# A weight ring kept past the end of the mixer, and VectorE's forming steps kept in program order

## The chip, the core and the metric

The kernel runs on one core of one Trainium2 chip. The metric is the device time of one execution in microseconds. Its engines are TensorE (PE, with its weight loads as PEld), VectorE (DVE), ScalarE (ACT), GpSimd (POOL) and SyncE (SP), which only issues transfers here.

## What is computed

One transformer layer over 512 tokens of width 1024, in float32:

```
xn = rms_norm(h);  proj = xn @ w_in
... four mixers (short conv, spatial gating, stick-breaking and forgetting attention) ...
h = h + (sum over mixers of sigmoid(gate) * (y @ w_branch)) @ w_out
g, u = split(rms_norm(h) @ w_ffn_in)        # 1024 -> 2 x 2816
h = h + (silu(g) * u) @ w_ffn_out           # 2816 -> 1024
```

The change touches the last two lines, the feed-forward part.

## The kernel before

Every matrix is held transposed, 128 rows to a tile, tokens along the free axis. A float32 product is made of three float32r products: each operand is split into a high part (ScalarE copies it, L181) and a low part (VectorE subtracts, L182), and TensorE forms high by high, high by low and low by high. Weights come in chunks of eight 128x128 units, 512 KB each. A chunk is loaded into a raw tile by a transfer on SP's queue, and split into `whi` and `wlo`, two rings of three tiles in `wpool`, which lives through the whole kernel. So ScalarE can split a chunk once TensorE is done with the chunk three before it.

**The mixer** takes its raw tiles from `rawp`, a ring of three that is opened inside the stack `mix`. Its last stage multiplies by w_out: eight output rows d, one chunk of weights each, 24 matmuls of 512 columns. After each row VectorE adds x (L766), ScalarE makes the high part for the feed-forward and the square (L770, L773), VectorE the low part and the sum of squares (L771, L774). Then `mix.close()` (L784) gives the memory of the mixer back, and two pools, `opool` and `ffn`, are opened over it.

**The feed-forward, plain stage** (L856 to L912): the first four hidden rows of 128, eight chunks. TensorE's instructions are kept in program order here. The first chunk's products with k below 6 come first, then the sums for the norm (`rms`), with the remaining products of the first row between its two steps. Between the products, `steps` of `operands` (L882) form the operands of the next stage.

**The superblocks** (L947, 13 of them): the remaining rows in 2x2 blocks by Winograd's form of Strassen's scheme, seven products instead of eight. A superblock loads four weight blocks, `b11`, `t1`, `b22`, `b21` (b11 is added into t1 by a GpSimd transfer that accumulates, L810), forms three sums of them on VectorE (L959, L971, L978) and splits seven weight operands. A product is 24 matmuls of 256 columns (L922 to L924). Nine superblocks are of kind "in" (two hidden rows each), four of kind "out". In their order, three "in" follow on each complete group of eight hidden rows before the first "out" of that group.

**The forming** makes the token operands of an "out" pair: `operands` gives eleven steps, seven that split a quarter (`operand`) and four that add or subtract quarters (`differ`, and the sum in L897). They stand in the list `forming`, and `form()` (L933) takes one at a time, at four places of each superblock. So in program order the eleven steps of a group lie over three superblocks. Program order is not what the engines run: a list scheduler arranges each engine's instructions by its own estimate of when they are ready, within the dependencies. `tc.keep_in_program_order` puts an instruction behind the instruction that was written before it on its engine.

**The end**: 48 units of w_ffn_out in plain products again (L1021), six chunks, loaded by `block` like the others.

In the feed-forward all raw tiles come from `block` (L805), a ring of six tiles named `sraw` in the pool `ffn`.

Of the kernel before, what the change touches and what calls it, by code (L numbers as in the profile page):

```python
# [11 lines left out]
F32 = mybir.dt.float32  # L12
F32R = mybir.dt.float32r
BF16 = mybir.dt.bfloat16
AF = mybir.ActivationFunctionType
ALU = mybir.AluOpType
AX = mybir.AxisListType

P = 128
# [12 lines left out]
PLAIN = 4  # L32
GROUP = 8
REST = 16

BLOCKS = 6
EPS = 1e-6
NEG = -1e30
UNITS = 8
# [84 lines left out]
def mixer_kernel(ctx, tc, xT, units, ffn_units, quads, wt1, wt2, wsT, small, out):  # L124
    nc = tc.nc
    V, S, G, PE = nc.vector, nc.scalar, nc.gpsimd, nc.tensor

    const = ctx.enter_context(tc.tile_pool(name="const", bufs=1))
    wpool = ctx.enter_context(tc.tile_pool(name="wpool", bufs=3))
    keep = ctx.enter_context(tc.tile_pool(name="keep", bufs=1))  # L130
    psum = ctx.enter_context(tc.tile_pool(name="psum", bufs=1, space=bass.MemoryType.PSUM))

    mix = ExitStack()
    fixed = mix.enter_context(tc.tile_pool(name="fixed", bufs=1))
    sm = mix.enter_context(tc.tile_pool(name="sm", bufs=4))
    rawp = mix.enter_context(tc.tile_pool(name="rawp", bufs=3))
    slots = mix.enter_context(tc.tile_pool(name="slots", bufs=1))

    BUFS = dict(y=18, att=4, aug=6, tmp=6, gt=4)
# [2 lines left out]
    def nm(p):  # L142
        uid[0] += 1
        return f"{p}_{uid[0]}"
# [29 lines left out]
    def bank(tag="g"):  # L174
        return psum.tile([P, T], F32, tag=tag, bufs=dict(g=3, a=5)[tag], name=nm("ps"))

    def f(t):
        return t.bitcast(F32)

    def split(dst_hi, dst_lo, src):  # L180
        S.activation(dst_hi, src, AF.Copy)  # L181
        V.tensor_tensor(dst_lo, src, f(dst_hi), op=ALU.subtract)  # L182
# [188 lines left out]
    for b in range(2):  # L371
        t = u2[:, b]
# [126 lines left out]
    for b in range(2):  # L499
        for c2 in range(2):  # L500
# [10 lines left out]
            for e in range(2):  # L511
                rows = slice(e * HD, (e + 1) * HD)
                src = ps.rearrange("p (c g t) -> p c g t", c=2, g=2)[rows, :, e, :]
                t = sm.tile([P, 2, P], F32, tag="mx", bufs=1, name=nm("mx"))
# [242 lines left out]
    for d in range(KT):  # L757
# [11 lines left out]
        hi, lo = x2[:, 0], x2[:, 1]  # L769
# [16 lines left out]
    ffn = ctx.enter_context(tc.tile_pool(name="ffn", bufs=1, reuse_waits="tile"))  # L786
# [15 lines left out]

    A = [quarter() for _ in range(2)]

    def block(src, add=None):  # L805

        t = ffn.tile([P, UNITS * P], F32, tag="sraw", bufs=BLOCKS, name=nm("sraw"))
        nc.sync.dma_start(out=t, in_=src)
        if add is not None:
            G.dma_start(out=t, in_=add, accum_op=ALU.add)  # L810
        return t
# [9 lines left out]
    def ffn_unit(expect):  # L821
        c, j = divmod(fpos[0], UNITS)
        assert FFN_STREAM[fpos[0]] == expect, (FFN_STREAM[fpos[0]], expect)
        fpos[0] += 1
        if j == 0:
            fpos[1] = parts(block(ffn_units[c]))
        return tuple(t[:, j * P:(j + 1) * P] for t in fpos[1])
# [14 lines left out]
    def plain_gate(ps):  # L842
        t = ftile("gt")
        V.tensor_tensor(t, ps, r2, op=ALU.mult)
        S.activation(t, t, AF.Silu)
        V.tensor_tensor(t, t, r2, op=ALU.mult)
        return t
# [33 lines left out]

    def operands(X, first, last, tile_of):  # L882

        a11, a21, a12, a22 = first[:, 0], first[:, 1], last[:, 0], last[:, 1]

        def operand(name, src):
            X[name] = tile_of(name), tile_of(name)
            split(*X[name], src)

        def differ(a, b, to):  # L890
            V.tensor_tensor(to, a, b, op=ALU.subtract)  # L891

        return [lambda: operand("11", a11), lambda: operand("22", a22),
                lambda: differ(a21, a22, a22), lambda: operand("s1", a22),
                lambda: differ(a11, a21, a21), lambda: differ(a22, a11, a11), lambda: operand("s2", a11),
                lambda: operand("12", a12), lambda: operand("s3", a21),
                lambda: V.tensor_tensor(a12, a12, a11, op=ALU.add), lambda: operand("s4", a12)]  # L897

    XIN, XOUT = {}, {}
    steps = operands(XIN, *A, op_tile)  # L900
    t = plain_gate(gp)
    for j in range(PLAIN):
        if j:
            gp = bank("g")
            plain_product(j * P, range(KT), gp)
            t = plain_gate(gp)
# [7 lines left out]
    def product(ps, src, x, first=False):  # L914

        (wh, wl), (xh, xl) = parts(src), x
        for jj in range(2):
            dst = ps[:, jj * H:(jj + 1) * H]
            for k in range(4):
                u = slice((jj * 4 + k) * P, (jj * 4 + k + 1) * P)  # L920
                ends = k == 3 and jj == 1
                PE.matmul(out=dst, lhsT=wh[:, u], rhs=xh[:, k], start=first and k == 0 and jj == 0, stop=False, skip_group_check=True)  # L922
                PE.matmul(out=dst, lhsT=wh[:, u], rhs=xl[:, k], start=False, stop=False, skip_group_check=True)  # L923
                PE.matmul(out=dst, lhsT=wl[:, u], rhs=xh[:, k], start=False, stop=ends, skip_group_check=True)  # L924

    def copied(ps):
        t = ftile("tmp")
        S.activation(t, ps, AF.Copy)
        return t
# [7 lines left out]
    def tokens_of(i):  # L937
        return XIN if SUPER[i][0] == "in" else XOUT[SUPER[i][1]]

    def begin(i):  # L940
        c = 4 * i
        b = block(quads[c]), block(quads[c + 1], quads[c]), block(quads[c + 2]), block(quads[c + 3])
        px = bank("a")
        product(px, b[0], tokens_of(i)["11"], True)
        begun[i] = b, px, copied(px)

    def superblock(i):  # L947
        if i not in begun:
            begin(i)
# [29 lines left out]
        if i + 1 < len(SUPER):  # L979
            begin(i + 1)  # L980
# [26 lines left out]
    for i, block_ in enumerate(SUPER):  # L1007
        if block_[0] == "in" and block_[1] % GROUP == 0 and block_[1]:
            first = block_[1] - GROUP
            XOUT[first] = {}  # L1010
            forming += operands(XOUT[first], hidden[first // 4], hidden[first // 4 + 1], group_tile)
        if block_[0] == "out":
            assert not forming
            if ("in", FK - 2) in SUPER[:i] and not rest:
                forming += [lambda j=j: last_rows(j) for j in range(REST, FK, 2)]
                rest[REST] = None
        superblock(i)
# [79 lines left out]
```

## Time and profile before

| | |
|---|---|
| median of three runs | 805.86 us (803.04 to 806.17) |
| the profiled execution | 806.18 us |
| its span, first to last instruction | 804.5 us |
| mean granted clock of TensorE | 0.989 |
| TensorE, VectorE, ScalarE busy | 97%, 73%, 49% |

The profiled execution's own time is 1.7 us longer than its span. Times in the trace count from the span's start. The mixer ends near 441 us, the superblocks begin near 494 us.

### The profile page before, as it was taken

The numbers are of one execution on the slowest core, as the hardware profiler recorded it, in microseconds if no ns is written. First come the engines' busy times: TensorE is split into PE (matmuls) and PEld (weight loads), VectorE is DVE, ScalarE is ACT, GpSimd is POOL, SyncE is SP. The second block draws the span as 40 slices with busy tenths as digits, with TensorE's granted clock in tenths as the row PEclk, the third lists the DMA queues.
The fourth block names the chain that finished last, engine by engine and source line by source line (L and its number), as shares of the span: only waits on it lengthen the run. The fifth ranks groups of instructions, "written<-read, shape, count | busy, mean of one in ns | idle before, by whom it ended". The sixth has DMA issues, their size and how long they took to land.

```text
span 804.5 us, 11458 instructions
## 1 busy us (share of the span) xinstructions
PE 784.0 (97%) x4607; PEld 689.3 (86%) x4607; DVE 584.3 (73%) x811; ACT 391.0 (49%) x541; POOL 19.8 (2%) x36
## 2 busy tenths in 40 slices
PE   8999999999999999999999999998999997999998
PEld 6888898888888888888887788998999996999987
DVE  8447886887786788737654598789778797788842
ACT  7336327667753445434343444566444554455420
POOL 1000000000000000000000000000000000000000
PEclk9999999999999999999999899999999998999999
DMA  7323222222222222243360342444354442444411
GB/s 281 131 79 117 80 79 79 79 80 78 79 79 82 91 80 68 88 143 106 105 236 0 108 128 48 124 119 131 115 139 134 134 128 80 136 135 131 132 39 66
DMA packets 25973, 85.84 MB, mean 107 GB/s; under 512 B 2880, under 2 KB 3136, under 8 KB 25920
## 3 DMA queue, kind: packets, MB, share of 16 engines
q1 hardware_dynamic: 22608, 75.80, 28.4%
q0 software_dynamic: 1872, 6.82, 5.2%
q10 hardware_dynamic: 1440, 2.49, 1.0%
q8 instruction: 36, 0.59, 0.3%
q14 instruction: 17, 0.14, 0.1%
HBM read 83.00 MB, written 2.10 MB: 106 GB/s over the span
## 4 chain that ended last, share of the span: by engine, by line
PE 93%; DVE 4%; ACT 1%; issue 1%; DMA 0%; SPq 0%; ACTq 0%; DVEq 0%
PE ps L188 54%; PE ps L924 10%; PE ps L923 10%; PE ps L922 10%; PE ps L199 1%; PE ps L197 1%; PE ps L198 1%; PE ps L538 1%; DVE wlo L182 1%; DVE xg L182 1%; PE ps L704 1%; DMA raw<-units 0%; ACT whi L181 0%; DVE part L891 0%; PE ps L688 0%
## 5 line engine op out<-in xcount | busy, mean ns | idle before, releaser
L188 PE MATMUL ps<-xg,whi 128*128 128x512 f32 x896 | 284.1, 397 | 3.9 <-ACT whi L181 3.9
L188 PEld LDWEIGHTS ps<-xg,whi 128*128 128x128 f32 x896 | 168.8, 190 | 41.6 <-ACT whi L181 5.1
L181 ACT ACTIVATE whi<-sraw 128x1024 fp32r<-128x1024 f32 x105 | 110.8, 1060 | 144.9 <-PE ps L923 66.4
L188 PE MATMUL ps<-xg,wlo 128*128 128x512 f32 x448 | 176.3, 399 | 0.5 <-DVE wlo L182 0.5
L182 DVE TENSOR_TENSOR wlo<-sraw,whi 128x1024 fp32r<-128x1024 f32 x105 | 127.9, 1224 | 50.7 <-ACT whi L181 50.5
L922 PE MATMUL ps<-op,whi 128*128 128x256 f32 x504 | 143.0, 285 | 4.7 <-ACT whi L181 3.8
L924 PE MATMUL ps<-op,wlo 128*128 128x256 f32 x504 | 140.2, 283 | 5.1 <-DVE wlo L182 5.1
L923 PE MATMUL ps<-op,whi 128*128 128x256 f32 x504 | 142.3, 283 | 0.0
L181 ACT ACTIVATE whi<-raw 128x1024 fp32r<-128x1024 f32 (+2 forms) x74 | 74.5, 1010 | 97.6 <-PE ps L188 78.8
L182 DVE TENSOR_TENSOR wlo<-raw,whi 128x1024 fp32r<-128x1024 f32 (+2 forms) x74 | 86.1, 1164 | 37.3 <-ACT whi L181 36.7
L188 PEld LDWEIGHTS ps<-xg,wlo 128*128 128x128 f32 x448 | 84.9, 189 | 19.9 <-DVE wlo L182 1.0
L922 PEld LDWEIGHTS ps<-op,whi 128*128 128x128 f32 x504 | 96.4, 191 | 5.8 <-ACT whi L181 4.7
L924 PEld LDWEIGHTS ps<-op,wlo 128*128 128x128 f32 x504 | 96.0, 193 | 5.6 <-DVE wlo L182 5.6
L923 PEld LDWEIGHTS ps<-op,whi 128*128 128x128 f32 x504 | 96.6, 192 | 0.0
L188 PE MATMUL ps<-y,whi 128*128 128x512 f32 x224 | 70.6, 395 | 0.0
L188 PEld LDWEIGHTS ps<-y,whi 128*128 128x128 f32 x224 | 42.0, 188 | 9.7
L188 PE MATMUL ps<-y,wlo 128*128 128x512 f32 x112 | 44.1, 394 | 0.0
L922 PE MATMUL ps<-xg,whi 128*128 128x256 f32 x128 | 36.1, 282 | 0.2 <-DVE gt L975 0.2
L923 PE MATMUL ps<-xg,whi 128*128 128x256 f32 x128 | 35.8, 280 | 0.0
L924 PE MATMUL ps<-xg,wlo 128*128 128x256 f32 x128 | 35.7, 279 | 0.0
L730 ACT ACTIVATE gt<-gt 128x512 f32<-128x512 f32 x32 | 20.1, 628 | 23.7 <-DVE gt L729 23.4
L188 PE MATMUL ps<-op,whi 128*128 128x512 f32 (+1 forms) x108 | 30.6, 370 | 1.0 <-ACT whi L181 1.0
(264 smaller groups left out, 1172.4 us busy)
## 6 DMA issues: line engine op xcount, KB each, us to landing
raw<-units SPq DMA_DIRECT2D x60, 512.0 KB, 3.3
sraw<-quads SPq DMA_DIRECT2D x52, 512.0 KB, 3.4
sraw<-ffn_units SPq DMA_DIRECT2D x14, 512.0 KB, 4.4
sraw<-quads POOLq DMA_DIRECT2D x13, 512.0 KB, 5.4
x<-xT SPq DMA_DIRECT2D x8, 256.5 KB, 5.3
raw<-units SPq DMA_DIRECT2D x8, 256.0 KB, 5.3
raw<-wt SPq DMA_DIRECT2D x4, 512.0 KB, 3.8
tmp<-xT ACTq DMA_DIRECT2D x8, 256.0 KB, 3.5
```

Source lines behind the costliest of these rows:

```text
L181: S.activation(dst_hi, src, AF.Copy)
L182: V.tensor_tensor(dst_lo, src, f(dst_hi), op=ALU.subtract)
L188: i = PE.matmul(**args)
L197: PE.matmul(out=ps, lhsT=ah, rhs=bh, start=start, stop=False)
L198: PE.matmul(out=ps, lhsT=al, rhs=bh, start=False, stop=False)
L199: PE.matmul(out=ps, lhsT=ah, rhs=bl, start=False, stop=stop)
L538: PE.matmul(out=pv[:, kb * P:], lhsT=v[:, kb, h].rearrange("p n c -> p (n c)"), rhs=w[:, cols(kb)], start=(kb == 0 and m == 0), stop=(kb = ...
L704: PE.transpose(out=tp[:, kb * P:(kb + 1) * P], in_=t[:, kb * P:(kb + 1) * P], identity=ident)
L730: S.activation(t, t, AF.Tanh, scale=0.5)
L922: PE.matmul(out=dst, lhsT=wh[:, u], rhs=xh[:, k], start=first and k == 0 and jj == 0, stop=False, skip_group_check=True)
L923: PE.matmul(out=dst, lhsT=wh[:, u], rhs=xl[:, k], start=False, stop=False, skip_group_check=True)
L924: PE.matmul(out=dst, lhsT=wl[:, u], rhs=xh[:, k], start=False, stop=ends, skip_group_check=True)
```

## The change

The pool `rawp` is opened outside `mix`, so it stays to the end. `block` takes its tile from that ring of three, but for two blocks of each superblock, `t1` and `b21`, which have a ring `sraw` of three in `ffn`. The memory is the same in sum. In `operands`, the low part of a token operand and the sums of quarters go through `differ`, which keeps them in program order on VectorE; ScalarE's copy for the high part is not kept so.

```
-BLOCKS = 6
...
     wpool = ctx.enter_context(tc.tile_pool(name="wpool", bufs=3))
+    rawp = ctx.enter_context(tc.tile_pool(name="rawp", bufs=3))
...
-    rawp = mix.enter_context(tc.tile_pool(name="rawp", bufs=3))
...
-    def block(src, add=None):
-        t = ffn.tile([P, UNITS * P], F32, tag="sraw", bufs=BLOCKS, name=nm("sraw"))
+    def block(src, add=None, own=False):
+        if own:
+            t = ffn.tile([P, UNITS * P], F32, tag="sraw", bufs=3, name=nm("sraw"))
+        else:
+            t = rawp.tile([P, UNITS * P], F32, tag="raw", name=nm("raw"))
...
         def operand(name, src):
-            X[name] = tile_of(name), tile_of(name)
-            split(*X[name], src)
-        def differ(a, b, to):
-            V.tensor_tensor(to, a, b, op=ALU.subtract)
+            X[name] = hi, lo = tile_of(name), tile_of(name)
+            S.activation(hi, src, AF.Copy)
+            differ(src, f(hi), lo)
+        def differ(a, b, to, op=ALU.subtract):
+            tc.keep_in_program_order(V.tensor_tensor(to, a, b, op=op))
...
-                lambda: V.tensor_tensor(a12, a12, a11, op=ALU.add), lambda: operand("s4", a12)]
+                lambda: differ(a12, a11, a12, ALU.add), lambda: operand("s4", a12)]
...
-        b = block(quads[c]), block(quads[c + 1], quads[c]), block(quads[c + 2]), block(quads[c + 3])
+        b = block(quads[c]), block(quads[c + 1], quads[c], True), block(quads[c + 2]), block(quads[c + 3], None, True)
```

## Rows read from the trace of the kernel before

**Rows 1.** The page's first part: each engine's busy time, share of span, instructions.

```profile
PE 784.0 (97%) x4607; PEld 689.3 (86%) x4607; DVE 584.3 (73%) x811; ACT 391.0 (49%) x541; POOL 19.8 (2%) x36
```

**Rows 2.** What PE waited for in the whole span: us in total, times, longest.

```profile
PE ps L924 <- DVE wlo L182: 5.1, 2, 3.1
PE ps L188 <- ACT whi L181: 5.0, 3, 3.0
PE ps L922 <- ACT whi L181: 3.8, 4, 2.3
```

**Rows 3.** Windows: busy us (instructions) of PE, PEld, DVE, ACT, POOL; clock; DMA.

```profile
400.00:440.00 40.00, 40.00 (x174) 32.30 (x173) 19.22 (x25) 14.99 (x21) 0.00 (x0) 1.00 0.36 131
440.00:460.00 20.00, 16.46 (x67) 12.87 (x66) 9.86 (x13) 8.01 (x11) 0.00 (x0) 0.83 0.32 106
```

**Rows 4.** PE's order of time around the boundary: start, us, instruction, idle before.

```profile
440.37 0.40 PE L188 MATMUL ps<-y,wlo 128*128 128x512 f32 x1
...
443.77 0.73 PE L188 MATMUL ps<-xg,whi 128*128 128x512 f32 x2 [3.00 <-ACT whi L181]
...
451.43 0.40 PE L188 MATMUL ps<-xg,wlo 128*128 128x512 f32 x1
```

**Rows 5.** SP's order of time, the first loads of the feed-forward.

```profile
410.38 1.96 SPq L808 DMA_DIRECT2D sraw<-ffn_units  x4
```

**Rows 6.** ACT's order of time at the boundary.

```profile
442.16 0.61 ACT L773 ACTIVATE tmp<-mrg 128x512 f32<-128x512 f32 x1
442.68 2.94 ACT L181 ACTIVATE whi<-sraw 128x1024 fp32r<-128x1024 f32 x3
```

**Rows 7.** DVE's order of time at the boundary.

```profile
424.93 1.23 DVE L182 TENSOR_TENSOR wlo<-raw,whi 128x1024 fp32r<-128x1024 f32 x1 [0.17 <-ACT whi L181]
...
429.63 0.69 DVE L766 TENSOR_TENSOR mrg<-ps,tmp 128x512 f32<-128x512 f32 x1 [2.22 <-PE ps L188]
...
443.75 3.50 DVE L182 TENSOR_TENSOR wlo<-sraw,whi 128x1024 fp32r<-128x1024 f32 x3
```

**Rows 8.** Equal windows with and without PE's gaps in the superblocks, columns as above.

```profile
532.90:567.40 34.50, 30.55 (x241) 29.73 (x240) 34.44 (x34) 19.64 (x22) 1.73 (x2) 0.95 0.38 94
567.40:601.90 34.50, 34.50 (x296) 34.50 (x296) 24.45 (x25) 17.92 (x23) 1.72 (x2) 1.00 0.50 141
637.90:676.10 38.20, 32.09 (x247) 31.14 (x246) 37.13 (x38) 18.56 (x21) 1.72 (x2) 0.92 0.35 86
676.10:714.30 38.20, 38.20 (x326) 38.20 (x325) 28.61 (x30) 20.89 (x26) 1.73 (x2) 1.00 0.49 138
```

**Rows 9.** DVE by lines, 532.9 to 567.4: count, busy, mean ns, idle before.

```profile
L182 DVE TENSOR_TENSOR wlo<-sraw,whi 128x1024 fp32r<-128x1024 f32 x10 | 12.1, 1229 | 0.0
L182 DVE TENSOR_TENSOR xg<-part,xg 128x1024 fp32r<-128x1024 f32 x4 | 4.9, 1226 | 0.0
...
L182 DVE TENSOR_TENSOR hop<-part,hop 128x1024 fp32r<-128x1024 f32 x2 | 2.5, 1229 | 0.0
...
L891 DVE TENSOR_TENSOR part<-part,part 128x1024 f32<-128x1024 f32 x2 | 2.5, 1226 | 0.0
```

**Rows 10.** DVE by lines, 567.4 to 601.9.

```profile
L182 DVE TENSOR_TENSOR wlo<-sraw,whi 128x1024 fp32r<-128x1024 f32 x12 | 14.7, 1224 | 9.2 <-ACT whi L181 9.2
```

**Rows 11.** DVE and PE in order of time where PE stops in the superblocks.

```profile
562.72 3.51 DVE L182 TENSOR_TENSOR wlo<-sraw,whi 128x1024 fp32r<-128x1024 f32 x3
...
564.01 0.58 PE L924 MATMUL ps<-op,wlo 128*128 128x256 f32 x1 [2.01 <-DVE wlo L182]
```

**Rows 12.** DVE in order of time, back to back.

```profile
539.83 0.69 DVE L993 TENSOR_TENSOR part<-gt,gt 128x512 f32<-128x512 f32 x1
540.43 1.22 DVE L891 TENSOR_TENSOR part<-part,part 128x1024 f32<-128x1024 f32 x1
541.57 1.23 DVE L182 TENSOR_TENSOR wlo<-sraw,whi 128x1024 fp32r<-128x1024 f32 x1
```

**Rows 13.** DMA issues on the page: count, size, median us to landing.

```profile
raw<-units SPq DMA_DIRECT2D x60, 512.0 KB, 3.3
```

## The prediction

> **What bounds the kernel now.** I read the page's first part first. TensorE is busy 97% of the span, VectorE 73%, ScalarE 49% [rows 1]. An average like this says that TensorE is the bound nearly everywhere, so a change can only give back what TensorE loses in a few places. The list of TensorE's waits says which. Almost all its waiting is for the two halves of a weight chunk, `whi` from ScalarE and `wlo` from VectorE, and it comes in a handful of waits of 2 to 3 us, not in many small ones [rows 2]. The windows then place them. 400 to 440 us is full; 440 to 460 us has 16.46 us of TensorE in 20, at a mean granted clock of 0.83 [rows 3]. The other two places are in the superblocks: two stretches of equal length beside each pair of windows, one with a hole and one without [rows 8]. So there are three holes. Each costs twice: the idle time, and behind it a stretch at the lower clock (1.2 instead of 2.4 GHz).
>
> *First hole, mixer to feed-forward.* The undisturbed pitch of a 512-column matmul is 40.00 us / 173 = 0.231 us (one of the 174 straddles the window's edge) [rows 3]. From the start of the last matmul of w_out at 440.37 to the start of the eighteenth of the feed-forward at 451.43 are 18 steps [rows 4]. They should take 18 x 0.231 = 4.2 us and take 11.1. **Loss 6.9 us.**
>
> *Second and third hole, superblocks.* 34.5 us hold 296 matmuls when undisturbed and 241 with the hole: 55 x 0.117 = 6.4 us. 38.2 us hold 326 and 247: 79 x 0.1175 = 9.3 us [rows 8]. That is 15.7 us. The trace may miss a few matmul records, so this is an upper bound. The lower one comes from idle time and clock. Second hole: 34.50 - 30.55 = 3.95 us idle, and a clock of 0.95 is half level in a tenth of the window, 3.5 us, half of it lost: 5.7. Third: 6.1 us idle, and of the clock's share I count nothing, as part of it falls into the idle time. Sum 11.8. I take **15 us**, near the count, because most of the slow stretch does run matmuls.
>
> **Why the first hole is there.** The first feed-forward transfer was issued at 410.38 [rows 5], some 30 us before the hole, and such a transfer lands in 3.3 us [rows 13]. So the weights were there. The slot in `wpool` was free too. For the last w_out chunk the split ran at 424.93, three rows of w_out ahead; by the same step the first feed-forward chunk could have been split once row 5 was done, which is where VectorE reads its sum, at 429.63 [rows 7]. Instead ScalarE makes three copies in a row directly behind the very last mixer instruction (442.16, then 442.68 with no idle time) and VectorE's three subtractions stand at 443.75 [rows 6, 7]. That is an order of issue, not a wait for data. My reading: `sraw` lies in a pool opened over memory of `mix`, and the scheduler places nothing that touches such a tile until the last instruction of `mix` is placed. The transfers show none of it, because on SP nothing stands between.
>
> **The change, part by part.**
>
> **The ring `rawp` outside `mix`.** With raw, `whi` and `wlo` all in pools that outlive `mix`, nothing ties the first splits to its end: chunk 0 can be split near 430, chunk 1 near 435, chunk 2 when row 7 is done. Then the eighteen matmuls follow at full pace. What is late next? The norm's sums need `hsum`, the last mixer instruction on VectorE, which is done before 443.75 [rows 7]; TensorE would want it at 440.6 + 4.2 = 444.8. It fits by about a microsecond. Gain 6.9 us; bounds 0 (order unchanged) and 6.9.
>
> **Three tiles ahead instead of six for the plain chunks.** A plain chunk feeds 24 matmuls, 24 x 0.231 = 5.5 us. A ring of three in the w_out stage, same chunk and same pace, leaves TensorE full, 40.00 of 40.00 [rows 3]; I cost it at nothing. Without that cover a chunk would be late by a landing, 3.3 us [rows 13], at each of 14.
>
> **Two rings of three in the superblocks.** One ring of six in the order b11, t1, b22, b21 reuses a tile six blocks later: b22 of the next superblock takes b11's, b21 takes t1's, b11 of the one after takes b22's, t1 takes b21's. Two rings of three pair exactly the same blocks. As many transfers, same queues, same additions: nothing.
>
> **VectorE's forming kept in order.** No instruction is added. What moves is the time. Back to back, a 1024-column instruction takes 541.57 - 540.43 = 1.14 us and a 512-column one 0.60 [rows 12]. An "in" superblock needs seven `wlo`, three weight sums and five small ones: 10 x 1.14 + 5 x 0.60 = 14.4 us of 168 x 0.1175 = 19.7. That leaves 5.3 idle, and the calm window agrees: 9.2 us of waiting for ScalarE in 1.75 superblocks [rows 10]. In the disturbed window VectorE never idles (34.44 of 34.50) [rows 8] and runs beside the ten `wlo` at least eight forming instructions [rows 9]: 1.75 x 14.4 + 8 x 1.14 = 34.3 us. The forming floated together, VectorE became the bound, and three `wlo` in a row end the wait of TensorE [rows 11]. In program order there are four per superblock: 14.4 + 4 x 1.14 = 19.0 of 19.7. VectorE fits, with 0.7 us to spare.
>
> It is tight, so what covers it? A split starts when a slot frees, two products ahead, 2 x 24 x 0.1175 = 5.6 us, and takes 0.98 (2.94 / 3 [rows 6]) + 1.23 [rows 9], so 3.4 us of slack per group of three superblocks. If a third of the 5.3 us of idle time stays, VectorE falls behind by (1.8 - 0.7) x 2.75 = 3.0, covered. If half stays, (2.6 - 0.7) x 2.75 = 5.2, and 1.8 us reach TensorE per group, more with the clock. The ends are 0 and the present 15; between them I take 2.5 us for both groups, as the calm waits are mostly VectorE being early. Gain 12.5.
>
> The Trainium skill speaks against this part. "VectorE: DVE Perf Modes" ("Terms", and "Side-by-side: where the cycles go") has every VectorE instruction drain its pipe before the next may issue, with some 158 cycles beside one element per cycle at 0.96 GHz. By that, an estimate, instructions would cost 1.23 and 0.70 us, a forming superblock 20.7 us, 1.0 more than TensorE's; with a third of the idle time left, (1.8 + 1.0) x 2.75 - 3.4 = 4.3 us per group would stay, 8.6 instead of 2.5 in all: 793 us. The rows differ: durations are 1.22, but starts are 1.14 apart, so I keep 1.14.
>
> **Sum.** 806.2 (profiled) - 6.9 - 15 + 2.5 = 786.8; the median of the runs is 0.3 below the profiled time. **Forecast 787 us.** Its own range is 783.5 (no residue, 15.7) to 790.
>
> **The rivals.**
>
> *The ring changes nothing.* The weights had landed long before; if the order of issue has another cause, the hole stays. For it: the landing. Against it: all engines start the feed-forward directly behind the last mixer instruction. 806.2 - 15 + 2.5 = 794. Chance 0.14.
>
> *VectorE stays the bound.* At 19.0 of 19.7 any lost microsecond is a lag: one of the two holes stays, or half of each. 806.2 - 6.9 - 7.5 = 792, to 798 with new slow stretches. For it: the margin of 0.7. Chance 0.17.
>
> *Only the ring works* and the forming floats as before: 806.2 - 6.9 = 799. Chance 0.04.
>
> *Slower, by a queue that blocks.* A pinned low part waits for ScalarE's copy of the same operand, and that copy can stand behind a `whi` copy that waits for a slot, up to one product, 24 x 0.1175 = 2.8 us. VectorE runs in order, so weight sums and `wlo` behind it wait too, and TensorE for them. All 14 low parts held 2.8 us are 39 us; margin and slack take 2 x (2.75 x 0.7 + 3.4) = 10.7, so 28 us reach TensorE: 784.3 + 28 = 812. It turns slower at 2.4 us each. Against it: ScalarE is half idle. Chance 0.05. The skill's "TensorE: Matmul & The Clock Gate" (on the array and queue depths) calls the queues of ScalarE and VectorE strict FIFO; the three `wlo` stuck behind other work [rows 11] agree.
>
> *It does not do what it says:* the scheduler lands near the old order, 802 to 806. Chance 0.05.
>
> **How the numbers follow.** The forecast has 0.55. 783 to 798 holds it, the first rival and most of the second: about 0.8. A measurement of this kernel tells 0.5%, 4 us, from no change. Faster by more: 0.55 + 0.14 + 0.17 + 0.04 = 0.90, less a little for mixed cases, 0.88. Same 0.06, slower 0.06.
>
> **What would show it.** Right: the first `whi` of the feed-forward near 430 on ScalarE and no wait of TensorE at 441; the clock 1.00 throughout; forming instructions spread over some 55 us, with VectorE at about 95% there. Wrong: a wait for `whi` at the boundary; VectorE at 100% for 20 us on end; VectorE idle in front of a `differ`, waiting for ScalarE; a transfer into `raw` that lands less than a split ahead of its use.

## The result and the profile after

| | before | after |
|---|---|---|
| median | 806.01 us (803.04 to 806.59, 4 runs) | 784.57 us (784.48 to 785.27, 4 runs) |
| span of the profiled execution | 804.5 us | 782.9 us |
| mean granted clock of TensorE | 0.989 | 1.0 |

The ratio is 0.9743, with a 95% interval of 0.9719 to 0.9768: 21.4 us faster. The page's first part of the changed kernel, each engine's busy time, share and instructions:

```profile
PE 776.4 (99%) x4607; PEld 683.6 (87%) x4607; DVE 582.8 (74%) x811; ACT 390.6 (50%) x541; POOL 19.8 (3%) x36
```

The count of instructions is the one of before [rows 1]; TensorE is busy for 7.6 us less in sum, since no matmul runs at the lower clock, and its share has gone from 97% to 99%. What TensorE still waits for (us in total, times, longest), but for two short waits in the mixer's part, 1.3 and 0.4 us here and 1.3 and 0.5 in before:

```profile
PE ps L186 <- ACT whi L179: 1.0, 1, 1.0
PE ps L928 <- DVE wlo L180: 0.6, 1, 0.6
```

The waits of 2 to 3 us [rows 2] are gone. The window that lost 3.54 us at a clock of 0.83 [rows 3], and the three superblocks in which the first group is formed, with a quiet one before and one after (columns as in [rows 3]):

```profile
440.00:460.00 20.00, 20.00 (x96) 16.52 (x95) 13.83 (x19) 9.59 (x13) 1.88 (x2) 1.00 0.70 195
```

```profile
512.00:531.80 19.80, 19.80 (x172) 19.80 (x171) 15.07 (x16) 10.72 (x13) 0.86 (x1) 1.00 0.50 134
531.80:551.50 19.70, 19.70 (x170) 19.70 (x169) 18.05 (x19) 11.94 (x15) 0.86 (x1) 1.00 0.50 134
551.50:571.20 19.70, 19.70 (x170) 19.70 (x169) 18.52 (x20) 11.71 (x14) 0.86 (x1) 1.00 0.50 134
571.20:590.90 19.70, 19.70 (x170) 19.70 (x170) 19.16 (x21) 11.26 (x14) 0.86 (x1) 1.00 0.50 135
...
610.60:630.00 19.40, 19.40 (x167) 19.40 (x166) 14.51 (x16) 10.95 (x13) 0.86 (x1) 1.00 0.52 136
```

TensorE is full in all of them. VectorE goes from 15.07 us of 19.8 to 18.05, 18.52 and 19.16 of 19.7 and by 610 us back to 14.51: heavily loaded, for three superblocks, but not at 100% as in the first disturbed window [rows 8]. In the second group it is at 100%, or nearly:

```profile
690.00:710.00 20.00, 20.00 (x172) 19.99 (x171) 19.73 (x21) 11.79 (x14) 0.86 (x1) 1.00 0.47 126
```

From 681.7 to 707.5 us VectorE has no idle time at all, because the low parts of the last hidden rows run beside the forming there. TensorE stays full until the wait of 0.6 us at 711 us. The instructions of `differ` in the first group, by form (count, duration, first and last start):

```profile
L895 DVE TENSOR_TENSOR xg<-part,xg x4: 1215/1216/1218, 539.1 to 583.7; 128x1024 fp32r<-128x1024 f32 x4
L895 DVE TENSOR_TENSOR hop<-part,hop x3: 1216/1217/1219, 526.5 to 564.0; 128x1024 fp32r<-128x1024 f32 x3
L895 DVE TENSOR_TENSOR part<-part,part x3: 1208/1209/1217, 541.3 to 579.2; 128x1024 f32<-128x1024 f32 x3
L895 DVE TENSOR_TENSOR part<-part x1: 1217/1217/1217, 546.2 to 546.2; 128x1024 f32<-128x1024 f32 x1
```

These are the eleven steps, from 526.5 to 583.7 us: 57 us. Before, ten of them stood in the 34.5 us of [rows 9], which leaves out these two lines:

```profile
L897 DVE TENSOR_TENSOR part<-part,part 128x1024 f32<-128x1024 f32 x1 | 1.2, 1233 | 0.0
L891 DVE TENSOR_TENSOR part<-part 128x1024 f32<-128x1024 f32 x1 | 1.2, 1229 | 0.0
```

These ten start between 537.6 and 559.9 us, within some 22 us.

At the end of the mixer ScalarE's order of time now reads:

```profile
429.94 1.06 ACT L179 ACTIVATE whi<-raw 128x1024 fp32r<-128x1024 f32 x1 [3.42 <-issue]
430.91 0.71 ACT L768 ACTIVATE xg<-mrg,g 128x512 fp32r<-128x512 f32 x1
...
435.51 1.06 ACT L179 ACTIVATE whi<-raw 128x1024 fp32r<-128x1024 f32 x1 [3.37 <-issue]
...
441.11 1.06 ACT L179 ACTIVATE whi<-raw 128x1024 fp32r<-128x1024 f32 x1 [1.89 <-issue]
442.07 0.71 ACT L768 ACTIVATE xg<-mrg,g 128x512 fp32r<-128x512 f32 x1
442.68 0.62 ACT L771 ACTIVATE tmp<-mrg 128x512 f32<-128x512 f32 x1
```

The copies of the first feed-forward chunks stand between the mixer's own (L768, L771 are L770, L773 of before), each as soon as a row of w_out is done, and not in a block behind the last of them [rows 6]. TensorE goes from the last matmul of w_out to the first of the feed-forward, and to the eighteenth, without a gap (compare [rows 4]):

```profile
440.86 0.39 PE L186 MATMUL ps<-y,wlo 128*128 128x512 f32 x1
...
441.09 0.62 PE L186 MATMUL ps<-xg,whi 128*128 128x512 f32 x2
...
445.04 0.39 PE L186 MATMUL ps<-xg,wlo 128*128 128x512 f32 x1
```

445.04 - 440.86 = 4.18 us for the eighteen steps that took 11.06 before.

### The profile page after: what moved, and what is told of

Same layout as the page of the kernel before. It is cut to its first block, busy times and chain, and to the rows that moved or that the text cites. A ratio compares the mean times of both kernels' runs of the same rounds, so it can differ in the third digit from the quotient of the medians.

```text
span 782.9 us, 11441 instructions
## 1 busy us (share of the span) xinstructions
PE 776.4 (99%) x4607; PEld 683.6 (87%) x4607; DVE 582.8 (74%) x811; ACT 390.6 (50%) x541; POOL 19.8 (3%) x36
## 4 chain that ended last, share of the span: by engine, by line
PE 98%; ACT 1%; DVE 0%; issue 0%
PE ps L186 55%; PE ps L927 11%; PE ps L926 11%; PE ps L928 11%; PE ps L197 1%; PE ps L196 1%; PE ps L195 1%; PE ps L536 1%; PE ps L702 1%; PE ps L238 1%; PE ps L686 0%; PE ps L602 0%; PE ps L569 0%; PE ps L601 0%; PE ps L687 0%
## 5 line engine op out<-in xcount | busy, mean ns | idle before, releaser
L179 ACT ACTIVATE whi<-raw 128x1024 fp32r<-128x1024 f32 (+2 forms) x127 | 130.8, 1031 | 197.3 <-PE ps L186 95.6
L180 DVE TENSOR_TENSOR wlo<-raw,whi 128x1024 fp32r<-128x1024 f32 (+2 forms) x127 | 150.7, 1188 | 67.5 <-ACT whi L179 67.1
L926 PE MATMUL ps<-op,whi 128*128 128x256 f32 x504 | 140.7, 281 | 0.0
L927 PE MATMUL ps<-op,whi 128*128 128x256 f32 x504 | 140.7, 281 | 0.0
L928 PE MATMUL ps<-op,wlo 128*128 128x256 f32 x504 | 138.3, 279 | 0.0
L927 PEld LDWEIGHTS ps<-op,whi 128*128 128x128 f32 x504 | 95.1, 189 | 0.0
L926 PEld LDWEIGHTS ps<-op,whi 128*128 128x128 f32 x504 | 95.0, 189 | 0.0
L928 PEld LDWEIGHTS ps<-op,wlo 128*128 128x128 f32 x504 | 93.9, 188 | 0.0
L179 ACT ACTIVATE whi<-sraw 128x1024 fp32r<-128x1024 f32 x52 | 54.6, 1060 | 45.0 <-DVE sraw L963 16.3
L180 DVE TENSOR_TENSOR wlo<-sraw,whi 128x1024 fp32r<-128x1024 f32 x52 | 62.6, 1219 | 6.9 <-ACT whi L179 6.9
```

## The experiments

### One half of the change at a time

The ring alone, the forming free:

```
         def operand(name, src):
-            X[name] = hi, lo = tile_of(name), tile_of(name)
-            S.activation(hi, src, AF.Copy)
-            differ(src, f(hi), lo)
+            X[name] = tile_of(name), tile_of(name)
+            split(*X[name], src)
...
-            tc.keep_in_program_order(V.tensor_tensor(to, a, b, op=op))
+            V.tensor_tensor(to, a, b, op=op)
```

> The ring kept past the mixer, the forming free as before. If the boundary hole and the two holes in the superblocks have separate causes, only the boundary hole goes: 806.0 - 6.9 = 799, with both later holes of TensorE still in the trace. If the ring has nothing to do with it (the weights were there long before), 806. If shifting the start also resolves the forming, 785.

Measured: 799.39 us beside 805.48 of before on the same chip, ratio 0.9922 (0.9907 to 0.9936), 6.1 us faster. Windows over the boundary and the superblocks (columns as above):

```profile
440.00:460.00 20.00, 20.00 (x96) 16.53 (x95) 14.00 (x19) 9.76 (x13) 1.88 (x2) 1.00 0.66 190
...
520.00:560.00 40.00, 36.01 (x297) 35.19 (x296) 37.41 (x38) 22.85 (x27) 1.73 (x2) 0.99 0.38 106
560.00:600.00 40.00, 40.00 (x333) 40.00 (x333) 29.88 (x31) 20.00 (x24) 1.72 (x2) 0.97 0.48 133
...
640.00:680.00 40.00, 34.18 (x268) 33.11 (x268) 34.94 (x36) 20.78 (x24) 1.73 (x2) 0.91 0.40 119
```

The boundary is full. 520 to 560 us and 640 to 680 us lose 3.99 and 5.82 us, with the clock below 1 behind them: the two holes of before [rows 8], 6.5 us earlier.

The order alone, as a diff to the kernel before, with its ring of six in the late pool:

```
-            X[name] = tile_of(name), tile_of(name)
-            split(*X[name], src)
+            X[name] = hi, lo = tile_of(name), tile_of(name)
+            S.activation(hi, src, AF.Copy)
+            differ(src, f(hi), lo)
-        def differ(a, b, to):
-            V.tensor_tensor(to, a, b, op=ALU.subtract)
+        def differ(a, b, to, op=ALU.subtract):
+            tc.keep_in_program_order(V.tensor_tensor(to, a, b, op=op))
...
-                lambda: V.tensor_tensor(a12, a12, a11, op=ALU.add), lambda: operand("s4", a12)]
+                lambda: differ(a12, a11, a12, ALU.add), lambda: operand("s4", a12)]
```

> The old ring of six in the late pool, the forming kept in order. Separate causes: the hole at the boundary stays with its 6.9 us, the two others go: 784.6 + 6.9 = 791.5. If the order alone is the whole gain, 785. If the forming needs the split rings too, above 795.

Measured: 789.68 us, ratio 0.9802 (0.9786 to 0.9819), 15.8 us faster than before and 5.1 above the changed kernel. ScalarE at the boundary, and the windows:

```profile
442.03 0.61 ACT L773 ACTIVATE tmp<-mrg 128x512 f32<-128x512 f32 x1
442.55 2.94 ACT L181 ACTIVATE whi<-sraw 128x1024 fp32r<-128x1024 f32 x3
```

```profile
440.00:460.00 20.00, 16.47 (x72) 13.01 (x71) 11.13 (x15) 8.98 (x12) 0.53 (x1) 0.91 0.32 106
...
520.00:560.00 40.00, 40.00 (x343) 40.00 (x342) 33.63 (x35) 22.63 (x27) 1.73 (x2) 1.00 0.46 132
560.00:600.00 40.00, 40.00 (x343) 40.00 (x342) 38.00 (x38) 23.14 (x28) 1.73 (x2) 1.00 0.48 133
...
640.00:680.00 40.00, 40.00 (x343) 40.00 (x342) 36.01 (x37) 22.11 (x27) 1.73 (x2) 1.00 0.45 123
```

The hole at the boundary is where it was, the superblocks are full. So the two halves repair different places and add up: 6.1 + 15.8 = 21.9, against 21.4 together.

### Why the first hole was there: the pool of the first raw tile

In the changed kernel, one line says which plain chunks take a tile of the late pool's ring `sraw`. First chunks 1 to 7 do and chunk 0 keeps the kept ring, then the reverse:

```
-            fpos[1] = parts(block(ffn_units[c]))
+            fpos[1] = parts(block(ffn_units[c], None, 0 < c < 2 * PLAIN))
```

```
-            fpos[1] = parts(block(ffn_units[c]))
+            fpos[1] = parts(block(ffn_units[c], None, c == 0))
```

> The changed kernel, but of the eight plain chunks only the first has its raw tile in the ring that outlives the mixer; the other seven use the ring of three in the late pool. If what matters is only that the first split touches no tile of the late pool, the hole stays away: 784.6 to 785.5, chunk 1 is split behind the last mixer instruction, just in time. If the lead of the whole ring is needed, part of the hole returns: 787 to 791.

Measured: 785.39 us, ratio 0.9747 (0.9733 to 0.9762), 0.8 above the changed kernel. One chunk in the kept ring is enough to remove the hole. ScalarE's order:

```profile
429.80 1.06 ACT L179 ACTIVATE whi<-raw 128x1024 fp32r<-128x1024 f32 x1 [3.42 <-issue]
430.77 0.70 ACT L768 ACTIVATE xg<-mrg,g 128x512 fp32r<-128x512 f32 x1
...
442.50 0.62 ACT L771 ACTIVATE tmp<-mrg 128x512 f32<-128x512 f32 x1
446.11 0.26 ACT L322 ACTIVATE rc<-ps,eps 128x4 f32<-128x4 f32 x1 [2.99 <-PE ps L186]
446.27 2.94 ACT L179 ACTIVATE whi<-sraw 128x1024 fp32r<-128x1024 f32 x3
```

Chunk 0 is copied at 429.80. The three next, with tiles of the late pool, follow in a block at 446.27, behind the last mixer instruction, and cost TensorE one wait of 0.5 us.

> The changed kernel, but the first plain chunk has its raw tile in the late pool, all others in the ring that outlives the mixer. If the pool of the first raw tile decides, the whole hole returns although seven of eight chunks are early: 784.6 + 6.9 = 791.5, and ScalarE's first copy stands behind the last mixer instruction. If the lead of the loads decides, 785.

Measured: 789.77 us, ratio 0.9804 (0.9789 to 0.9818): the same as with no kept ring at all. SP's and ScalarE's order:

```profile
414.96 11.53 SPq L810 DMA_DIRECT2D raw<-ffn_units  x3
426.54 0.42 SPq L810 DMA_DIRECT2D sraw<-ffn_units  x1
```

```profile
442.14 0.61 ACT L771 ACTIVATE tmp<-mrg 128x512 f32<-128x512 f32 x1
442.66 1.04 ACT L179 ACTIVATE whi<-sraw 128x1024 fp32r<-128x1024 f32 x1
443.61 1.99 ACT L179 ACTIVATE whi<-raw 128x1024 fp32r<-128x1024 f32 x2
```

Three chunks are loaded early into the kept ring, from 414.96 on, and chunk 0 into the late pool at 426.54, 16 us before its copy. None of this helps: its copy stands right behind the last mixer instruction, and the copies of the early chunks stand behind it. What decides is not the lead of the loads but in which pool the first raw tile lies.

### Why the other two holes were there: VectorE's work in front of the low parts

The order kept, but two steps at each place:

```
     def form():
-        if forming:
-            forming.pop(0)()
+        for _ in range(2):
+            if forming:
+                forming.pop(0)()
```

> The changed kernel, order kept, but two forming steps at each of the four places of a superblock, so that the eleven steps lie over six places instead of eleven. If VectorE's load makes the holes, they return in spite of the kept order: a superblock then needs 14.4 + 8 x 1.14 = 23.5 us of VectorE against 19.7 of TensorE, a lag of 3.8 x 1.4 = 5.3 us, less 3.4 of slack, per group: 2 us each, up to twice that with the slower clock: 788 to 793. If the disorder itself made the holes and not the load, 785.

Measured: 793.73 us, ratio 0.986 (0.9845 to 0.9875), 9.2 us above the changed kernel and 0.7 above the upper end of what was expected of the load. Windows of one superblock each, and TensorE's longest wait in the first group:

```profile
531.80:551.50 19.70, 19.70 (x170) 19.70 (x169) 19.28 (x20) 12.90 (x17) 0.86 (x1) 1.00 0.48 134
551.50:571.20 19.70, 16.83 (x129) 16.56 (x128) 17.40 (x18) 9.12 (x12) 0.86 (x1) 0.91 0.32 106
571.20:590.90 19.70, 19.70 (x170) 19.70 (x169) 14.94 (x16) 10.00 (x12) 0.86 (x1) 1.00 0.50 138
```

```profile
555.73 0.39 PE L928 MATMUL ps<-op,wlo 128*128 128x256 f32 x1 [2.87 <-DVE wlo L180]
```

VectorE is at 19.28 of 19.7 in the first superblock, and in the next TensorE stops for 2.87 us waiting for a `wlo`, with the clock at 0.91 over that window. The second group has the same hole, a wait of 2.88 us. In the changed kernel the two windows of the first group are full. So a kept order does not by itself keep TensorE fed; the spacing does.

But the trace does not show the lag over a whole superblock that was expected. VectorE still idles for 0.42 us until 549.8, waiting for TensorE. Then two steps in a row stand in front of the `wlo` that TensorE needs, and take 2.3 us, as in the second group:

```profile
552.18 1.22 DVE L895 TENSOR_TENSOR hop<-part,hop 128x1024 fp32r<-128x1024 f32 x1
553.32 1.22 DVE L895 TENSOR_TENSOR xg<-part,xg 128x1024 fp32r<-128x1024 f32 x1
554.46 2.35 DVE L180 TENSOR_TENSOR wlo<-sraw,whi 128x1024 fp32r<-128x1024 f32 x2
```

And VectorE without idle time is not yet a hole: in the changed kernel it works for 26 us on end from 681.7, and TensorE waits 0.6 us. So the run shows that steps standing together make a hole though their order is kept. How much of the two holes of before is such a pile in front of a low part, and how much VectorE's load over the whole stretch, no run separates.

TensorE's waits for ScalarE's `whi` in the kernel before [rows 2] lead back to VectorE too. In the third hole ScalarE's copies waited for a weight sum:

```profile
665.80 2.00 ACT L181 ACTIVATE whi<-sraw 128x1024 fp32r<-128x1024 f32 x2 [1.87 <-DVE sraw L959]
```

Half of the order, first only the four sums, then only the seven low parts:

```
-            X[name] = hi, lo = tile_of(name), tile_of(name)
-            S.activation(hi, src, AF.Copy)
-            differ(src, f(hi), lo)
+            X[name] = tile_of(name), tile_of(name)
+            split(*X[name], src)
```

```
-            differ(src, f(hi), lo)
+            tc.keep_in_program_order(V.tensor_tensor(lo, src, f(hi), op=ALU.subtract))
...
-            tc.keep_in_program_order(V.tensor_tensor(to, a, b, op=op))
+            V.tensor_tensor(to, a, b, op=op)
```

> Only the four sums of quarters kept in order; the seven low parts are free. Four of the low parts depend on a kept sum, so only three (11, 22 and 12) can run ahead: 785 to 787. If the low parts are what floats, 791 to 799.

> Only the seven low parts kept in order; the four sums are free. A group then packs at most four instructions early, 4.6 us of VectorE against 3.4 of slack and 5.3 of idle time: 785 to 787. If the sums are what floats and blocks, 791 to 799.

Measured: 785.33 us, ratio 0.9753 (0.9739 to 0.9768), and 785.42 us, ratio 0.9754 (0.9737 to 0.977). Either half does nearly all of it, 0.8 and 0.9 us above the changed kernel. TensorE's waits account for that: in place of the 0.6 us there are 1.5 us for `wlo` with the sums kept, and 1.6 us for a copy of ScalarE (`tmp`, L932) with the low parts kept. My reading is that the steps hang together by their data, so that a chain kept at some of its links stays spread; no run tests that by itself.

### The two waits that are left

Beside the second group's forming VectorE also makes the low parts of the last six hidden rows (`last_rows`), which the change leaves free. Keeping them in order too, and TensorE's matmuls of the last stage:

```
-        split(*(t.rearrange("p j h t -> p h j t") for t in (hi, lo)), hidden[j // 4][:, :, j % 4:j % 4 + 2])
+        th, tl = (t.rearrange("p j h t -> p h j t") for t in (hi, lo))
+        src = hidden[j // 4][:, :, j % 4:j % 4 + 2]
+        S.activation(th, src, AF.Copy)
+        tc.keep_in_program_order(V.tensor_tensor(tl, src, f(th), op=ALU.subtract))
...
+    pinned[0] = True
     for d in range(KT):
```

> The changed kernel, and the same order also for the low parts of the last six hidden rows on VectorE (they run beside the second group's forming at 684 to 714 us) and for TensorE's matmuls of the last stage. The two waits of TensorE that are left, 0.6 and 1.0 us, go: 784.6 - 1.6 = 783.0. If order costs overlap at the end, 785 or more.

Measured: 783.99 us, ratio 0.9736 (0.9722 to 0.9751), 1.0 above the expected 783.0. The two waits were gone but a new one of 1.6 us stood at 720 to 740 us. Then the changed kernel and each edit by itself, on one chip:

> The changed kernel itself, on the same chip as the two beside it, for a base: 784.6.

> The changed kernel with TensorE's matmuls of the last stage in program order, nothing else. The wait of 1.0 us for the last stage's first chunk goes, the one of 0.6 us stays: 1.0 us below the changed kernel. If other work waits in its place, no difference.

> The changed kernel with the low parts of the last six hidden rows in program order, nothing else. The wait of 0.6 us beside the second group's forming goes; the run with both edits showed a new one of 1.6 us later, which comes from here: 0.5 to 1.0 us above the changed kernel. If that wait came from the matmuls' order, 0.6 below.

Measured: 784.71 us (784.30 to 785.03) for the changed kernel, 784.95 (784.62 to 785.08) with the last stage's matmuls kept, 783.76 (783.60 to 783.88) with the low parts kept; ratios to before 0.9742 (0.9723 to 0.976), 0.9744 (0.9726 to 0.9763) and 0.9729 (0.971 to 0.9747). TensorE's waits, first with the matmuls kept, then with the low parts kept:

```profile
PE ps L926 <- ACT tmp L932: 1.5, 1, 1.5
...
PE ps L928 <- DVE wlo L180: 0.6, 1, 0.6
```

```profile
PE ps L186 <- ACT whi L179: 1.1, 1, 1.1
```

I had put the new wait down to the wrong edit. It comes from the matmuls' order. In the changed kernel four early matmuls of the last stage run in that place, at 740.4 us, behind the wait of 1.0 us for their chunk. Kept behind the superblocks they cannot, and TensorE waits there for the copy `tmp` instead; the times of the two versions overlap, so no gain is shown for that edit. The low parts in order remove the 0.6 us beside the second group and bring nothing new. That version is the fastest here: 0.95 us below the changed kernel, with ranges that do not touch, though the intervals of their ratios to before overlap. Of the 0.95 us the wait explains 0.6; the rest is open.

## Why the prediction was right, and the size that was off

**Where TensorE loses time.** Three holes, each with its slow stretch: shown. Elsewhere TensorE's idle time changed by the new wait of 0.6 us and by 0.9 us in the first 100 us, where two runs of the changed kernel differ by 0.5 us as well.

**The first hole is an order of issue, not a late load.** Shown twice: chunk 0 alone in the kept ring removes it, chunk 0 alone in the late pool brings it back, with the weights of its followers in place for long. That the scheduler will not place an instruction on a tile of a pool before the last instruction of the pool under it is placed, is the reading that fits all four runs; no run tests the scheduler's rule itself. Both late pools are opened with `reuse_waits="tile"`, and whether that setting has a part in the order was not tested either. The first five feed-forward transfers took 4.2 to 9.3 us to land, not the 3.3 of the mixer's, which still leaves them 20 us early. The rival by which the ring changes nothing falls with the ring's own 6.1 us. The 6.9 us of the prediction were those of the one profiled execution; alone the ring gave 6.1, and taking it away from the changed kernel cost 5.1.

The two later holes, taken at 15 us between 11.8 and 15.7, gave 15.8 by the order alone, residue and all. That is already above the 15.7 that was called an upper bound. In the two profiled executions the time from the start of the eighteenth matmul to the end of the span went from 353.1 to 337.9 us, 15.2 less, again with the residue in it. So the count of matmuls was the better measure. That the forecast of 787 came within 2.5 us is in part luck: the first hole and the residue were taken too high, the later holes too low.

**What is late next.** `hsum` was to fit by about a microsecond. Its last addition (L772) starts at 444.00 us and lasts 0.68, and TensorE wants it at 445.27: 0.6 us to spare.

**Rings of three, and half of the blocks.** Costed at nothing, and no wait of TensorE in the changed kernel is for a transfer. The run with chunks 1 to 7 in the ring of the late pool fed from three tiles too.

**The forming.** The price of VectorE was about right. The three windows of the first group hold three, three and four steps, and 14.4 us and 1.14 a step make 17.8, 17.8 and 19.0; 18.05, 18.52 and 19.16 were measured. The prediction's check on that price in the disturbed window agreed by luck. It took 1.75 superblocks and eight steps, 34.3 us. The window holds ten steps, and its ten `wlo` are those of 1.43 superblocks, since TensorE stood still in it: 26 instructions at 1.14 and 8 at 0.60, 34.4 us.

The term that was off is the residue, which I took at 2.5 us between 0 and 15: it is one wait of 0.6 us, at the end of the second group, where `last_rows` adds to the load. With the residue at 0.6 the sum is 784.3 + 0.6 = 784.9, and 784.57 was measured. I had let a third to a half of VectorE's idle time stay. It did not. My reading is that most of it was VectorE being early, waiting for ScalarE's `whi` [rows 10], and that a busier VectorE stops being early; in the second group it had no idle time left for 26 us. "VectorE at 100% for 20 us on end", which the prediction names as a sign of being wrong, is therefore there, and went with 0.6 us of waiting.

**The rivals.** VectorE as the bound is real, but not with one step at each place: with two it came, and 793.7. The Trainium skill's rule in "VectorE: DVE Perf Modes" (Terms), that each instruction drains before the next may issue, would have put four steps over TensorE's time, by the prediction's estimate 20.7 us against 19.7. The trace after says no once more: two of `differ` in a row at 572.92 take 2.35 us, 1.13 for the first and 1.22 for the second. The slower rival, kept instructions that block VectorE's queue, did not appear: in the trace of the changed kernel VectorE never sits idle in front of a `differ`.

## What to carry to other kernels

When an engine's copies or splits stand in a block right behind the last instruction of a stage although their data came long before, ask in which pool their tiles lie: one tile, for the first chunk, in a pool that outlives the stage was enough here. When VectorE is near 75% busy on average, work that is ready early may have to be spread by hand over the stretch in which it must be done; left free, the scheduler packed it here, and TensorE paid for the lump twice, in waiting and in clock. Spread means one step at a time: two in a row in front of what TensorE needed next were enough for a wait of 2.9 us. Before costing what such a spread leaves over, look at why the engine idles: here nearly all the idle time could be filled.

## What the runs showed of the hardware that was not expected

The same hole does not cost the same. TensorE idled 3.0 and 0.5 us at the boundary in before, in the run with the order alone and in the run with all but chunk 0. But behind it the granted clock over 444 to 452 us was 0.57 in before and 0.79 in the two others. First before, then the order alone:

```profile
444.00:452.00 8.00, 7.47 (x22) 5.59 (x21) 3.25 (x3) 1.61 (x2) 0.00 (x0) 0.57 0.58 197
```

```profile
444.00:452.00 8.00, 7.47 (x30) 5.86 (x29) 3.29 (x4) 1.75 (x3) 0.00 (x0) 0.79 0.59 197
```

With the order alone the matmuls are back at a pitch of 0.23 us from 448.9 us on, in before only from about 451. By the eighteen steps the hole cost 6.9 us in before, 5.6 with the order alone and 5.3 with all but chunk 0, with the same matmuls in front of it. Runs of the kernel before differ among themselves in the same sense, from 802.92 us at a mean clock of 0.994 to 806.66 at 0.987. Why the higher level returned sooner stays open.
